# Edge rows stored apart, value products for two query blocks at once, and K and V projected earlier

## The chip, the cores and the metric

One core of one Trainium2 chip runs the whole program. Its engines work side by side, each through its own queue in order: TensorE (PE) multiplies matrices, VectorE (DVE) and ScalarE (ACT) work on elements, GpSimd (POOL) and SyncE (SP) here mainly issue DMA transfers. The metric is device time in microseconds from launch to end, lower is better; it is the median of several executions.

## The reference

Two requests (512 and 256 tokens, 768 in all) pass through two encoder layers with shared weights. All is float32. Cut to what matters:

```
h = rms_norm(x, norm_g);  u = h @ w_in            # 2048 -> 46 column blocks of 128 (and dt)
z, xbc, dt_raw, q, k, v, g_att, hy_proj, g_hy = split(u)
y_ssd = ssd_branch(...)      # conv, two chunked scans (forward, backward), gate z, norm
y_att = attention_branch(...)  # 8 heads, 2 key/value heads, blocks of 128, window 128, bias, sink
y_hy  = hyena_branch(...)    # conv, long filters by Fourier transforms, gate, norm
x = x + concat(y_ssd, y_att, y_hy) @ w_out        # 16 column blocks of 128

# one scan, per chunk of 128 tokens and head
a_cs   = cumsum(dt * a)
y_diag = (C B^T * exp(a_cs_l - a_cs_s) masked) (x dt)
y_off  = (C . state before the chunk) * exp(a_cs)
# attention, per block of 128 queries against up to 3 blocks of keys
p = exp(s - max);  o = (p / (sum p + exp(sink - max))) @ v
```

## The kernel before

**Projections.** A column block is `gemm_col(W(i), f)`: 96 matmuls of 128x384 into two PSUM tiles (`gs`, `gq`), after which `f` takes the result. Each float32 operand is split into a high and a low part and three products are added. The activations' parts (`OPH`, `OPL`) stay in SBUF; the weights arrive on SP's queue (`raw`) and are split chunk by chunk, `hi` on ACT (recorded as L138) and `lo` on DVE (L128), with three buffers each. A chunk feeds 12 matmuls, so PE needs a new `hi` about every 2 us of its wide matmuls, and a late `hi` stops it.

**Background work.** Scan, Fourier filters, hyena and attention are Python generators that the class of `half`, `step`, `later` and `flush` advances between chunks of a column: a `half` step in the middle of a quarter runs due timers (`later`) and the functions that were put in the list `mid`, a whole `step` also advances the generators. `flush(gen)` runs a generator to its end at once. What is written down in this way is then put in an order per engine by the scheduler of the build, which sets the weight splits ahead.

**Scan.** The sixteen heads are handled as eight pairs a layer, beside the xs and hyena columns (W4 to W19). `a_cs` rows are written to `rows_d` in DRAM (six stores a layer, L638) and read back spread over the partitions: `rows` (L684, 256 KB each, six a pair) and, for the four chunks that have a neighbour before or after, `E2` (L726, per direction one load of three chunks, 192 KB, and one of one chunk, 64 KB). Then `xs_d` (L746, 385 KB) follows on the same GpSimd queue. ACT takes the exponent of each `E2`, DVE multiplies it with `Y`; the pair's last stage adds up on DVE `D x + y` and the `E2` terms into `XS`. The shared PSUM tiles `m` have four buffers, so a late `E2` holds `Y`, and with it the next pair's `Y`.

**Later columns.** After the scan come z (W20 to W27), whose squares end in `rms`, and `scale_ssd`, which scales the eight `XS` and stores them to `ys_d` (L1037, 384 KB each). Then the hyena's xa columns (W28 to W31), each behind `bg.flush(hy[j // 2])`; then K (W32), V (W33) and the four Q columns (W34 to W37), beside which attention runs. K's consumer writes `KH` by four ACT copies into the space of `XS` 6 and 7, so those wait for the `ys_d` stores to have read it.

**Attention.** A unit is one block of 128 queries of two heads; there are 24 a layer. They pass a pipeline: `score`, `turn` (transposes on PE), `pv`, which multiplies with the values (four or six instructions in the code, each two records in the trace, of the form 128*64 128x128), with one DVE copy behind it.

Of the kernel before, what the change touches and what calls it, by code (L numbers as in the profile page):

```python
# [11 lines left out]
F32 = mybir.dt.float32  # L12
# [7 lines left out]
DEPTH = 2  # L20
# [77 lines left out]
def trunk(ctx: ExitStack, tc: tile.TileContext, xT, w_in, w_dt, w_out, prm, brow, w1, mlpv, w2, w3, w4,  # L98
# [28 lines left out]
    def TT(o, a, b, op, eng=None):  # L127
        (eng or nc.vector).tensor_tensor(out=o, in0=a, in1=b, op=op)  # L128
# [5 lines left out]
    def STT(o, a, s, b, op0, op1, eng=None):  # L134
        (eng or nc.vector).scalar_tensor_tensor(out=o, in0=a, scalar=s, in1=b, op0=op0, op1=op1)  # L135
# [44 lines left out]
    fb_d = drp.tile([8, 128, 512], F32, name="fb_d")  # L180
    f0_d = drp.tile([8, 512], F32, name="f0_d")
    rows_d = drp.tile([DEPTH, 2, 16, NCH, 128], F32, name="rows_d")
    ys_d = drp.tile([DEPTH, 8, 128, T], F32, name="ys_d")
    xs_d = drp.tile([DEPTH, 8, 128, T + GAP], F32, name="xs_d")

# [2 lines left out]
    def P(l, base, i):  # L188
        c = l * NPRM + base + i
        return prm_t[:, c:c + 1]  # L190
# [413 lines left out]
    def ssd_gen(l, dtT, BT, CT, ready):  # L604
# [22 lines left out]
        TT(adt, dt, bc(na, (128, 2, NCH, 16)), MUL)  # L627
        yield
        yield
        for b in range(3):  # L630
            p = mp((16, 4, 128))
            for i in range(4):
                c, d = divmod(4 * b + i, 2)
                MM(p[:, i, :], adt[:, d, c, :], tri_t[:, d, :])
            r = t2((16, 4, 128))
            nc.scalar.copy(out=r, in_=p)
            for d in range(2):
                load(out=rows_d[l, d, :, 2 * b:2 * b + 2, :],  # L638
                     in_=r.rearrange("h (c d) t -> h d c t", d=2)[:, d])
        p = mp((128, 2, 2, NCH, 16))  # L640
        for d in range(2):
            MM(p[:, 0, d], tri_t[:, d, :], adt[:, d])
# [10 lines left out]
        TS(acs[:, 1], acs[:, 1], -1.0, MUL)  # L653
        yield
        yield

        FW, BW = (0, 1, 2, 4), (1, 2, 3, 5)

        def group(g):
            bt, cbF, cbB = s3((128, NCH, 128)), s3((128, NCH, 128)), s3((128, NCH, 128))  # L660
# [13 lines left out]
        def pair(j, bt, cbF, cbB):  # L674
            g, h0 = j // 4, 2 * j
            Xf = XS(j)
            X = Xf.rearrange("p (c h q) -> p c h q", c=NCH, h=2)
            Ms = []

            def rows(u):  # L680
                R = []
                for d in range(2):
                    t = t2((128, 2, 2, 128))
                    load(out=t, in_=rows_d[l, d, h0:h0 + 2, 2 * u:2 * u + 2, :].partition_broadcast(128))  # L684
                    R.append(t)
                return R

            def prep(u, R):
                Rf, Rb = R
                a1 = t2((128, 2, 2, 128))  # L690
                hc = [(hh, cc, h0 + hh, 2 * u + cc) for hh in range(2) for cc in range(2)]
                for hh, cc, h, c in hc:
                    STT(Rf[:, hh, cc, :], Rf[:, hh, cc, :], acs[:, 0, c, h:h + 1], Rb[:, hh, cc, :], SUB, ALU.min)
                for hh, cc, h, c in hc:
                    ACT(a1[:, hh, cc, :], cbF[:, c, :], AF.Copy, scale=dt[:, 0, c, h:h + 1])
                    ACT(Rb[:, hh, cc, :], cbB[:, c, :], AF.Copy, scale=dt[:, 1, c, h:h + 1])
                    ACT(Rf[:, hh, cc, :], Rf[:, hh, cc, :], AF.Exp, bias=acs[:, 1, c, h:h + 1])
                TT(Rb, Rb, a1, ADD)
                TT(Rf, Rf, Rb, MUL)
                Ms.append(Rf)  # L700

            R0 = rows(0)
            yield
            XW = []
            for d, cs in ((0, FW), (1, BW)):
                o = t2((128, 4, 2, 64))
                for i, n in ((0, 3), (3, 1)):
                    c = cs[i]
                    TT(o[:, i:i + n], X[:, c:c + n], bc(w[:, d, c:c + n, h0:h0 + 2][:, :, :, None], (128, n, 2, 64)), MUL)
                XW.append(o)  # L710
            R1 = rows(1)
            yield
            St = []
            for d, cs in ((0, FW), (1, BW)):
                p = mp((128, 4, 2, 64))
                for i, c in enumerate(cs):
                    MM(p[:, i], bt[:, c, :], XW[d][:, i])
                St.append(p)
            prep(0, R0)
            R2 = rows(2)  # L720
            E2 = []
            for d, cs in ((0, BW), (1, FW)):
                t = t2((128, 4, 128))
                for i, n in ((0, 3), (3, 1)):
                    src = rows_d[l, d, h0:h0 + 2, cs[i]:cs[i] + n, :]
                    load(out=t[:, i:i + n, :], in_=bass.AP(src.tensor, src.offset,  # L726
                         [[NCH * 128, 2], [0, 64], [128, n], [1, 128]]))
                E2.append(t)
            yield
            H = [t2((128, 4, 2, 64)), t2((128, 4, 2, 64))]  # L730
            nc.scalar.copy(out=H[0][:, 0:4:3], in_=St[0][:, 0:4:3])
            nc.scalar.copy(out=H[1][:, 2:4], in_=St[1][:, 2:4])
            for d, seq in ((0, ((1, 0, 1), (2, 1, 2))), (1, ((1, 2, 2), (0, 1, 1)))):
                for o, i, c in seq:
                    for hh in range(2):
                        STT(H[d][:, o, hh, :], H[d][:, i, hh, :], cdec[:, d, c, h0 + hh:h0 + hh + 1], St[d][:, o, hh, :], MUL, ADD)
            prep(1, R1)
            yield
            Y = []
            for d, cs in ((0, BW), (1, FW)):  # L740
                p = mp((128, 4, 128))
                for i, c in enumerate(cs):
                    MM(p[:, i, :], H[d][:, i], CT[g][:, tok(c)])
                Y.append(p)
            t = s3((128, T + GAP))
            load(out=t, in_=xs_d[l, j])  # L746
            prep(2, R2)
            yield
            for d in range(2):
                ACT(E2[d], E2[d], AF.Exp)  # L750
                TT(E2[d], E2[d], Y[d], MUL)
            yield
            yS, yP = mp((128, 4, 128)), mp((128, 2, 128))
            for c in range(NCH):
                for hh in range(2):
                    hs = slice(64 * hh, 64 * hh + 64)
                    o = yS[hs, c, :] if c < 4 else yP[hs, c - 4, :]
                    MM(o, X[:, c, hh, :], Ms[c // 2][:, hh, c % 2, :])
            yield
            dsk = P(l, PDS, j)  # L760
            yT = Xf.rearrange("p (c t) -> p c t", c=NCH)
            STT(yT[:, 0:4], t[:, 0:SL].rearrange("p (c t) -> p c t", c=4), dsk, yS, MUL, ADD)
            STT(yT[:, 4:6], t[:, SL + GAP:T + GAP].rearrange("p (c t) -> p c t", c=2), dsk, yP, MUL, ADD)
            for d, cs in ((0, BW), (1, FW)):
                for i, n in ((0, 3), (3, 1)):
                    c = cs[i]
                    TT(yT[:, c:c + n], yT[:, c:c + n], E2[d][:, i:i + n], ADD)
            yield

        act, nxt, gt = [], 0, None  # L770
# [23 lines left out]
    def att_gen(l, qs, QA, KH, KL, vt):  # L794
# [54 lines left out]
            for (w, _), (p, _) in zip(whole, pw):  # L849
                nc.scalar.copy(out=w, in_=p)  # L850

        def pv(i, tk, kb0, nk, whole, s):
            po = mp((128, 128))
            n = nk // 128
            for kb in range(n):
                for g in range(2):
                    hs = slice(64 * g, 64 * g + 64)
                    MM(po[hs, :], vt[:, kb0 + kb, hs], s[g][:, 128 * kb:128 * kb + 128], kb == 0, kb == n - 1)
            nc.vector.tensor_copy(out=qs[i][:, tk], in_=po)

        pipe = [None] * 4
        for u in units + [None] * 4:
            while u is not None and len(qs) <= u[0]:
                yield
            if pipe[3] is not None:
                pv(*pipe[3])
            if pipe[1] is not None:
                bg.mid.append(lambda p=pipe[1]: turn(*p))
            pipe = [score(*u) if u is not None else None] + pipe[:3]
            yield  # L870
# [96 lines left out]
    for l in range(DEPTH):  # L967
# [68 lines left out]
                TT(y, y, r, MUL)  # L1036
                load(out=ys_d[l, j], in_=y)  # L1037
        rms(acc, 1024, eps4, 2, scale_ssd)
        for j in range(4):
            def f(ps, pq):  # L1040
                bg.flush(hy[j // 2])
                a = hconv(j, ps, pq)
                TT(yh[j][:, 0:SL], yh[j][:, 0:SL], a[:, 0:SL], MUL)
                TT(yh[j][:, SL:T], yh[j][:, SL:T], a[:, SL + GAP:T + GAP], MUL)
            gemm_col(W(28 + j), f)

        new_xs(F32R)
        KH = [XS(6), XS(7)]
        kL = s3p.tile([128, T], F32R, tag="s3", name="kL")
        KL = [(kL[:, 0:SL], kL[:, SL:T]), (t2((128, SL), F32R), t2((128, PL), F32R))]  # L1050

        def f(ps, pq):
            k = s3()
            evac(lambda a, b: k[:, a:b], ps, pq, rstd)
            for g in range(2):
# [10 lines left out]
        def f(ps, pq):  # L1066
# [8 lines left out]
                    nc.scalar.copy(out=vt[:, 3 * b:3 * b + 3, :], in_=p)  # L1075
            bg.later(4, turn)
        gemm_col(W(33), f)
        qs, QA = [], [[XS(2 * i % 6), XS(2 * i % 6 + 1)] for i in range(4)]
        bg.add(att_gen(l, qs, QA, KH, KL, vt))
        for i in range(4):  # L1080
# [193 lines left out]
```

## Time and profile before

| | |
|---|---|
| time, median of 3 runs | 2487.45 us (2485.87 to 2487.83) |
| the profiled execution | 2489.0 us, span 2487.2 us |
| mean granted TensorE clock | 0.993 |
| PE busy | 2441.4 us (98%), 15066 matmul records |
| DVE, ACT, POOL busy | 1580.5, 1087.5, 341.4 us (64%, 44%, 14%) |
| DMA | 266.22 MB, mean 107 GB/s |

The trace is one execution. Its views are: the page; the waits (what ended an engine's idle time); the chain of waits (the work that ended last, followed back); the timeline of one engine, where a row with a count joins equal instructions, and the text in brackets is the idle time just before and what ended it; the DMA issues with the median time from issue to landing; and stretches (windows) with the busy time of each engine and the granted clock of PE (1.00 is 2.4 GHz, 0.50 is 1.2 GHz). The starts on PE are measured, the ends are modelled, so lengths of stretches on PE are taken from start to start.

### The profile page before, as it was taken

How to read it: one execution, taken by the hardware profiler on the slowest of the kernel's cores; microseconds unless marked ns; L12 is line 12 of the kernel's file. 1: busy time of each engine (PE TensorE's matmuls, PEld its weight loads, DVE VectorE, ACT ScalarE, POOL GpSimd, SP SyncE). 2: the span in 40 equal slices, each digit the busy share in tenths (PEclk: the TensorE clock that was granted, in tenths of full speed). 3: DMA queues.
4: the chain of work that ended last, by engine and by line, in shares of the span. 5: the costliest groups of instructions: out<-in, count | busy, mean ns of one | idle time of the engine just before them, and what ended most of it. 6: DMA issues, size and time to landing. Idle time of an engine off the chain costs nothing.

```text
span 2487.2 us, 40924 instructions
## 1 busy us (share of the span) xinstructions
PE 2441.4 (98%) x15066; PEld 2393.2 (96%) x15066; DVE 1580.5 (64%) x3410; ACT 1087.5 (44%) x2560; POOL 341.4 (14%) x683
## 2 busy tenths in 40 slices
PE   8999999999999999999999999999999999999998
PEld 7999999999999999999999999999999999999997
DVE  6888775558856766544476787766746477573333
ACT  6467653334334444333353575633332355352332
POOL 2033221221100010121200332201001000000001
PEclk9999999999999999999999999999999999999999
DMA  4266542443421132344421555423213111332223
GB/s 169 63 153 146 142 129 86 129 133 124 140 78 60 51 100 80 112 149 132 146 96 55 141 149 149 135 85 106 94 60 128 63 54 47 106 109 89 77 82 132
DMA packets 126921, 266.22 MB, mean 107 GB/s; under 512 B 30175, under 2 KB 36666, under 8 KB 126720
## 3 DMA queue, kind: packets, MB, share of 16 engines
q1 hardware_dynamic: 78048, 136.35, 17.7%
q0 software_dynamic: 48672, 127.26, 17.2%
q8 instruction: 118, 1.93, 0.3%
q14 instruction: 83, 0.68, 0.1%
HBM read 231.23 MB, written 34.18 MB: 107 GB/s over the span
## 4 chain that ended last, share of the span: by engine, by line
PE 90%; DMA 4%; issue 2%; DVE 1%; ACT 1%; POOL 1%; DVEq 0%; ACTq 0%; POOLq 0%
PE gs L141 38%; PE gq L141 38%; PE m L141 12%; DMA t<-rows_d 3%; PE m L848 1%; PE gl L141 1%; POOL t L726 0%; ACT t L138 0%; DMA XS<-in_xT 0%; DMA s<-in_xT 0%; ACT hi L138 0%; DVE lo L128 0%; DVE t L135 0%; PE m L1000 0%; DVE t L128 0%
## 5 line engine op out<-in xcount | busy, mean ns | idle before, releaser
L138 ACT ACTIVATE hi<-raw 128x256 fp32r<-128x256 f32 x984 | 405.6, 414 | 1040.1 <-PE gq L141 920.5
L128 DVE TENSOR_TENSOR lo<-raw,hi 128x256 fp32r<-128x256 f32 x984 | 412.5, 421 | 597.9 <-ACT hi L138 587.0
L141 PE MATMUL gs<-OPH,hi 128*128 128x384 f32 x1920 | 657.4, 342 | 18.1 <-ACT OPH L138 11.0
L141 PE MATMUL gs<-OPH,lo 128*128 128x384 f32 x1920 | 645.0, 336 | 0.6 <-DVE lo L128 0.5
L141 PE MATMUL gq<-OPH,lo 128*128 128x384 f32 x1920 | 644.4, 336 | 0.0
L141 PE MATMUL gs<-OPL,hi 128*128 128x384 f32 x1920 | 644.0, 336 | 0.1
L141 PE MATMUL gq<-OPH,hi 128*128 128x384 f32 x1920 | 644.1, 335 | 0.0
L141 PE MATMUL gq<-OPL,hi 128*128 128x384 f32 x1920 | 643.3, 335 | 0.0
L141 PEld LDWEIGHTS gs<-OPH,hi 128*128 128x128 f32 x1920 | 362.4, 189 | 25.2 <-ACT OPH L138 11.3
L141 PEld LDWEIGHTS gs<-OPH,lo 128*128 128x128 f32 x1920 | 361.6, 188 | 2.7 <-DVE lo L128 2.7
L141 PEld LDWEIGHTS gs<-OPL,hi 128*128 128x128 f32 x1920 | 362.3, 189 | 0.8 <-DVE OPL L135 0.6
L141 PEld LDWEIGHTS gq<-OPH,hi 128*128 128x128 f32 x1920 | 361.8, 188 | 0.0
L141 PEld LDWEIGHTS gq<-OPL,hi 128*128 128x128 f32 x1920 | 361.6, 188 | 0.0
L141 PEld LDWEIGHTS gq<-OPH,lo 128*128 128x128 f32 x1920 | 361.5, 188 | 0.0
L128 DVE TENSOR_TENSOR t<-t,t 128x512 f32<-128x512 f32 (+3 forms) x260 | 169.1, 668 | 26.5 <-ACT t L138 23.6
L135 DVE SCALAR_TENSOR_TENSOR s<-cv,prm_t,s 128x770 f32<-128x770 f32 x144 | 145.9, 1015 | 22.6 <-ACT s L138 21.9
L138 ACT ACTIVATE t<-s,dt 128x128 f32<-128x128 f32 x384 | 133.6, 391 | 18.9 <-DVE t L135 18.5
L128 DVE TENSOR_TENSOR s<-s,s 128x768 f32<-128x768 f32 (+2 forms) x126 | 112.8, 904 | 27.3 <-ACT s L138 26.7
L138 ACT ACTIVATE t<-t 128x512 fp32r<-128x512 f32 (+3 forms) x132 | 77.3, 587 | 92.4 <-DMA t<-rows_d 48.6
L128 DVE TENSOR_TENSOR t<-m,t 128x256 f32<-128x256 f32 (+3 forms) x157 | 72.3, 485 | 18.3 <-PE m L141 5.8
L684 POOL DMA_DIRECT2D t<-rows_d x96 | 68.8, 719 | 103.9 <-DVE XS L128 38.0
L138 ACT ACTIVATE t<-t,acs 128x128 f32<-128x128 f32 x192 | 73.6, 389 | 13.6 <-DVE t L135 13.6
(225 smaller groups left out, 2572.6 us busy)
## 6 DMA issues: line engine op xcount, KB each, us to landing
raw<-in_w_in SPq DMA_DIRECT2D x368, 256.0 KB, 3.0
raw<-in_w_out SPq DMA_DIRECT2D x128, 256.0 KB, 3.0
t<-rows_d POOLq DMA_DIRECT2D x96, 256.0 KB, 6.4
s<-in_xT POOLq DMA_DIRECT2D x24, 384.0 KB, 4.4
xs_d<-s POOLq DMA_DIRECT2D x16, 385.0 KB, 4.2
s<-xs_d POOLq DMA_DIRECT2D x16, 385.0 KB, 9.3
t<-rows_d POOLq DMA_DIRECT2D x32, 192.0 KB, 10.5
t<-in_decay POOLq DMA_DIRECT2D x24, 256.0 KB, 4.9
```

The costliest lines, as they stand in the source:

```text
L128: (eng or nc.vector).tensor_tensor(out=o, in0=a, in1=b, op=op)
L135: (eng or nc.vector).scalar_tensor_tensor(out=o, in0=a, scalar=s, in1=b, op0=op0, op1=op1)
L138: nc.scalar.activation(o, i, f, **kw)
L141: nc.tensor.matmul(o, lhsT=l, rhs=r, start=start, stop=stop)
L684: load(out=t, in_=rows_d[l, d, h0:h0 + 2, 2 * u:2 * u + 2, :].partition_broadcast(128))
L848: nc.tensor.transpose(pt[g][:, 128 * kb:128 * kb + 128], s[g][:, 128 * kb:128 * kb + 128], ident)
```

## The change

Five edits in one diff:

- a second DRAM array `ed_d` holds the four edge chunks of each direction; each of the six stores of a layer to `rows_d` gets a second store of one or two chunks beside it;
- an `E2` tile is loaded by two loads of 64 partitions x 2 KB from `ed_d`, one per head, instead of one of three chunks and one of one chunk over 128 partitions;
- the pair's last stage becomes a function in `bg.mid`;
- `pv2` gathers two units, multiplies both into one PSUM tile and copies each out;
- K and V are projected ahead of the xa columns, and `KH` and `KL` are allocated in K's consumer.

```diff
+    ed_d = drp.tile([DEPTH, 2, 16, 4, 128], F32, name="ed_d")
...
+        FW, BW = (0, 1, 2, 4), (1, 2, 3, 5)
         for b in range(3):
...
             for d in range(2):
-                load(out=rows_d[l, d, :, 2 * b:2 * b + 2, :],
-                     in_=r.rearrange("h (c d) t -> h d c t", d=2)[:, d])
+                v = r.rearrange("h (c d) t -> h d c t", d=2)[:, d]
+                load(out=rows_d[l, d, :, 2 * b:2 * b + 2, :], in_=v)
+                cs = [(i, c - 2 * b) for i, c in enumerate((BW, FW)[d]) if c // 2 == b]
+                i, c = cs[0]
+                load(out=ed_d[l, d, :, i:i + len(cs), :], in_=v[:, c:c + len(cs)])
...
-            for d, cs in ((0, BW), (1, FW)):
+            for d in range(2):
                 t = t2((128, 4, 128))
-                for i, n in ((0, 3), (3, 1)):
-                    src = rows_d[l, d, h0:h0 + 2, cs[i]:cs[i] + n, :]
-                    load(out=t[:, i:i + n, :], in_=bass.AP(src.tensor, src.offset,
-                         [[NCH * 128, 2], [0, 64], [128, n], [1, 128]]))
+                for hh in range(2):
+                    load(out=t[64 * hh:64 * hh + 64], in_=ed_d[l, d, h0 + hh].partition_broadcast(64))
...
-            yield
-            dsk = P(l, PDS, j)
...
+            def final():
+                dsk = P(l, PDS, j)
...
+            bg.mid.append(final)
             yield
...
-        def pv(i, tk, kb0, nk, whole, s):
-            po = mp((128, 128))
+        def pv2(us):
+            po = mp((128, len(us), 128))
+            for k, u in enumerate(us):
+                pv(po[:, k], *u)
+            for k, u in enumerate(us):
+                nc.vector.tensor_copy(out=qs[u[0]][:, u[1]], in_=po[:, k])
+
+        def pv(po, i, tk, kb0, nk, whole, s):
...
             if pipe[3] is not None:
-                pv(*pipe[3])
+                done.append(pipe[3])
+                if len(done) == 2:
+                    pv2(done)
+                    done = []
...
-        for j in range(4):
-            def f(ps, pq):
-                bg.flush(hy[j // 2])
...
-            gemm_col(W(28 + j), f)
-
-        new_xs(F32R)
-        KH = [XS(6), XS(7)]
...
+        KH, KL = [], []
 
         def f(ps, pq):
+            new_xs(F32R)
+            KH.extend((XS(6), XS(7)))
...
         gemm_col(W(33), f)
+        for j in range(4):
+            def f(ps, pq):
+                bg.flush(hy[j // 2])
...
+            gemm_col(W(28 + j), f)
+
```

The edits move instructions in three places. The first is attention on PE in layer 0, beside the Q columns; `gs` and `gq` are the wide projection matmuls, `64x128` the value products, `m<-XS`, `m<-kL` and the `128x256` row between or behind them the next unit's scores. Before, every gap between wide matmuls holds one unit's value products and a unit's scores:

```order
L141 MATMUL gq<-OPL,hi 128x384
L141 MATMUL gq<-OPH,lo 128x384
L141 MATMUL m<-t_8202,s_7829 64x128 x4
L141 MATMUL m<-XS 128x256
L141 MATMUL m<-kL,XS 128x256
L141 MATMUL m<-XS 128x256
L141 MATMUL m<-t_7675,XS 128x256
L141 MATMUL gs<-OPH,hi 128x384
```

Now one gap holds scores alone, and the next, one unit later, the value products of two units (four and six instructions) ahead of the scores:

```order
L141 MATMUL gq<-OPH,lo 128x384
L141 MATMUL m<-t_8209,s_6960 64x128 x4
L141 MATMUL m<-t_8263,s_6960 64x128
L141 MATMUL m<-t_8264,s_6960 64x128
L141 MATMUL m<-t_8263,s_6960 64x128
L141 MATMUL m<-t_8264,s_6960 64x128
L141 MATMUL m<-t_8263,s_6960 64x128
L141 MATMUL m<-t_8264,s_6960 64x128
L141 MATMUL m<-XS 128x256
L141 MATMUL m<-kL,XS 128x256
L141 MATMUL m<-XS 128x256
L141 MATMUL m<-t_6944,XS 128x256
```

The first unit's four products have moved to where the second's six stand; 22 gaps of the two layers lose their value products in this way.

The second place is the end of the hyena in layer 0 on PE; `m<-r,t` are the products that transform back into time. Before, the last 48 of them stand in one block behind the last matmul of column W31, ahead of column W32:

```order
L141 MATMUL gq<-OPL,hi 128x384
L141 MATMUL gq<-OPH,lo 128x384
L141 MATMUL m<-r_7436,t_7285 128x256 x2
L141 MATMUL m<-r_7437,t_7285 128x256
L141 MATMUL m<-r_7436,t_7286 128x256
L141 MATMUL m<-r_7436,t_7289 128x256
L141 MATMUL m<-r_7437,t_7289 128x256
```

Now they stand inside the column of W30, with two wide matmuls of it between them:

```order
L141 MATMUL gs<-OPH,hi 128x384
L141 MATMUL m<-r_7499,t_7255 128x256 x2
L141 MATMUL gs<-OPL,hi 128x384
L141 MATMUL gs<-OPH,lo 128x384
L141 MATMUL m<-r_7500,t_7255 128x256
L141 MATMUL m<-r_7499,t_7256 128x256
L141 MATMUL m<-r_7499,t_7259 128x256
L141 MATMUL m<-r_7500,t_7259 128x256
L141 MATMUL m<-r_7499,t_7260 128x256
L141 MATMUL m<-r_7505,t_7487 128x256
L141 MATMUL m<-r_7500,t_7255 128x256
L141 MATMUL m<-r_7506,t_7487 128x256
```

Column W30 is now the fifth behind the z columns where it was the third, so the hyena's generator has come to this stage before its flush.

The third place is the four `KH` copies on ACT in layer 0 (`XS<-s 64x768`) among the weight splits. Before, they stand about three columns behind the `ys_d` stores and wait for what was left of them:

```order
L138 ACTIVATE hi<-raw 128x256 [waits DVE_49,PE_49]
L138 ACTIVATE hi<-raw 128x256 [waits DMAHW5_49,DVE_49,PE_49]
L138 ACTIVATE XS<-s_7814 64x768 [waits DMASW7_49,DMASW0_49,DVE_49]
L138 ACTIVATE XS<-s_7814 64x768
L138 ACTIVATE hi<-raw 128x256 [waits PE_49,Activation_49]
L138 ACTIVATE XS<-s_7814 64x768 x2
L138 ACTIVATE hi<-raw 128x256 [waits DMAHW6_49,PE_49,Activation_49]
```

Now the first of them stands about one column behind the stores and waits for all eight (the eight DMASW semaphores), with the following splits queued behind it:

```order
L138 ACTIVATE hi<-raw 128x256 [waits DMAHW0_49,DVE_49,PE_49]
L138 ACTIVATE hi<-raw 128x256 [waits DVE_49,PE_49]
L138 ACTIVATE XS<-s_6945 64x768 [waits DMASW4_49,DMASW3_49,DMASW5_49,DMASW2_49,DMASW6_49,DMASW1_49,DMASW7_49,DMASW0_49,DVE_49]
L138 ACTIVATE XS<-s_6945 64x768 x2
L138 ACTIVATE hi<-raw 128x256 [waits DMAHW1_49,PE_49,Activation_49]
L138 ACTIVATE XS<-s_6945 64x768
L138 ACTIVATE hi<-raw 128x256 [waits PE_49,Activation_49]
```

What moved is the four copies, two columns ahead, so that the splits of the column behind V now stand behind the wait.

## Rows read from the trace of the kernel before

**Rows 1.** The page, the chain that ended last, by line.

```profile
PE gs L141 38%; PE gq L141 38%; PE m L141 12%; DMA t<-rows_d 3%; PE m L848 1%; PE gl L141 1%; POOL t L726 0%; ACT t L138 0%; DMA XS<-in_xT 0%; DMA s<-in_xT 0%; ACT hi L138 0%; DVE lo L128 0%; DVE t L135 0%; PE m L1000 0%; DVE t L128 0%
```

**Rows 2.** Waits of PE: waiter, releaser, us in total, times, longest.

```profile
PE m L141 <- DVE XS L135: 7.9, 2, 4.0
PE gs L141 <- ACT hi L138: 6.5, 5, 2.1
```

**Rows 3.** Chain of waits, 262 to 280 us: start, us, what.

```profile
264.84 9.33 DMA t<-rows_d
...
275.56 0.75 DVE XS L135
```

**Rows 4.** The E2 loads, line L726: who waited for them, and their landing.

```profile
ACT t L138: 48.6, 24
...
DMA to landing us min/median/max: 5.9/10.3/13.7
```

**Rows 5.** Timeline of PE around column W31's end: start, us, instruction, idle before.

```profile
690.70 0.34 PE L141 MATMUL gq<-OPH,lo 128*128 128x384 f32 x1
695.61 8.94 PE L141 MATMUL m<-r,t 128*128 128x256 f32 x48 [4.58 <-ACT r L138]
704.38 0.34 PE L141 MATMUL gs<-OPH,hi 128*128 128x384 f32 x1
```

**Rows 6.** Windows behind stalls: stretch, length, busy of five engines, PEclk, DMA, GB/s.

```profile
189.90:193.40 3.50, 3.47 (x11) 3.21 (x12) 3.47 (x9) 3.50 (x11) 0.00 (x0) 0.52 0.22 75
276.00:282.00 6.00, 5.64 (x23) 5.64 (x24) 4.84 (x14) 2.75 (x8) 0.72 (x1) 0.50 0.31 84
1528.00:1532.00 4.00, 4.00 (x17) 4.00 (x17) 2.84 (x8) 1.95 (x5) 0.64 (x1) 0.59 0.44 129
```

**Rows 7.** DMA issues of the page: queue, count, KB each, median us to landing.

```profile
t<-rows_d POOLq DMA_DIRECT2D x96, 256.0 KB, 6.4
...
s<-xs_d POOLq DMA_DIRECT2D x16, 385.0 KB, 9.3
...
t<-in_fwS POOLq DMA_DIRECT2D x32, 128.0 KB, 4.2
```

**Rows 8.** DMA issues, 1603 to 1605 us: the last xs_d load.

```profile
s<-xs_d POOLq DMA_DIRECT2D x1, 385.0 KB, 3.6
```

**Rows 9.** Timeline of POOL: the last five rows_d stores of layer 1.

```profile
1370.73 2.51 POOL L638 DMA_DIRECT2D rows_d<-t  x5 [0.92 <-issue]
```

**Rows 10.** Timeline of PE at one unit's and at two units' value products.

```profile
910.97 0.33 PE L141 MATMUL gq<-OPL,hi 128*128 128x384 f32 x1
911.14 0.34 PE L141 MATMUL gq<-OPH,lo 128*128 128x384 f32 x1
911.41 0.66 PE L141 MATMUL m<-t,s 128*64 128x128 f32 x8
...
912.28 0.34 PE L141 MATMUL gs<-OPL,hi 128*128 128x384 f32 x1
...
916.55 0.34 PE L141 MATMUL gq<-OPH,lo 128*128 128x384 f32 x1
916.82 1.13 PE L141 MATMUL m<-t,s 128*64 128x128 f32 x16
...
918.15 0.34 PE L141 MATMUL gs<-OPL,hi 128*128 128x384 f32 x1
```

**Rows 11.** Timeline of PE in column W28: the same products inside a column.

```profile
619.57 5.59 PE L141 MATMUL m<-r,t 128*128 128x256 f32 x46
```

**Rows 12.** Timeline of POOL: the last ys_d store of layer 0.

```profile
646.05 0.54 POOL L1037 DMA_DIRECT2D ys_d<-XS  x1 [0.67 <-PE gq L141]
```

**Rows 13.** The ys_d stores, line L1037: their landing.

```profile
DMA to landing us min/median/max: 3.3/4.8/7.1
```

**Rows 14.** The page: the weight splits on ACT, count, busy, mean ns, idle before.

```profile
L138 ACT ACTIVATE hi<-raw 128x256 fp32r<-128x256 f32 x984 | 405.6, 414 | 1040.1 <-PE gq L141 920.5
```

**Rows 15.** Timeline of PE: the first wide matmul of column W30.

```profile
648.54 0.33 PE L141 MATMUL gs<-OPH,hi 128*128 128x384 f32 x1
```

More of the change, by code (lines that the diff above doesn't have):

```diff
@@ L655, in ssd_gen @@
         yield
-        FW, BW = (0, 1, 2, 4), (1, 2, 3, 5)
         def group(g):
@@ L758, in pair @@
                     MM(o, X[:, c, hh, :], Ms[c // 2][:, hh, c % 2, :])
-            yield
-            dsk = P(l, PDS, j)
[L761 to L767, printed above, removed]
+            def final():
+                dsk = P(l, PDS, j)
+                yT = Xf.rearrange("p (c t) -> p c t", c=NCH)
+                STT(yT[:, 0:4], t[:, 0:SL].rearrange("p (c t) -> p c t", c=4), dsk, yS, MUL, ADD)
+                STT(yT[:, 4:6], t[:, SL + GAP:T + GAP].rearrange("p (c t) -> p c t", c=2), dsk, yP, MUL, ADD)
+                for d, cs in ((0, BW), (1, FW)):
+                    for i, n in ((0, 3), (3, 1)):
+                        c = cs[i]
+                        TT(yT[:, c:c + n], yT[:, c:c + n], E2[d][:, i:i + n], ADD)
+            bg.mid.append(final)
             yield
@@ L858, in pv @@
                     MM(po[hs, :], vt[:, kb0 + kb, hs], s[g][:, 128 * kb:128 * kb + 128], kb == 0, kb == n - 1)
-            nc.vector.tensor_copy(out=qs[i][:, tk], in_=po)
-        pipe = [None] * 4
+        pipe, done = [None] * 4, []
         for u in units + [None] * 4:
@@ L1038, in trunk @@
         rms(acc, 1024, eps4, 2, scale_ssd)
-        for j in range(4):
-            def f(ps, pq):
-                bg.flush(hy[j // 2])
-                a = hconv(j, ps, pq)
-                TT(yh[j][:, 0:SL], yh[j][:, 0:SL], a[:, 0:SL], MUL)
-                TT(yh[j][:, SL:T], yh[j][:, SL:T], a[:, SL + GAP:T + GAP], MUL)
-            gemm_col(W(28 + j), f)
-        new_xs(F32R)
-        KH = [XS(6), XS(7)]
-        kL = s3p.tile([128, T], F32R, tag="s3", name="kL")
-        KL = [(kL[:, 0:SL], kL[:, SL:T]), (t2((128, SL), F32R), t2((128, PL), F32R))]
+        KH, KL = [], []
         def f(ps, pq):
+            new_xs(F32R)
+            KH.extend((XS(6), XS(7)))
+            kL = s3p.tile([128, T], F32R, tag="s3", name="kL")
+            KL.extend(((kL[:, 0:SL], kL[:, SL:T]), (t2((128, SL), F32R), t2((128, PL), F32R))))
             k = s3()
@@ L1077, in trunk @@
         gemm_col(W(33), f)
+        for j in range(4):
+            def f(ps, pq):
+                bg.flush(hy[j // 2])
+                a = hconv(j, ps, pq)
+                TT(yh[j][:, 0:SL], yh[j][:, 0:SL], a[:, 0:SL], MUL)
+                TT(yh[j][:, SL:T], yh[j][:, SL:T], a[:, SL + GAP:T + GAP], MUL)
+            gemm_col(W(28 + j), f)
         qs, QA = [], [[XS(2 * i % 6), XS(2 * i % 6 + 1)] for i in range(4)]
```

## The prediction

> **What bounds the kernel now.** I read the page first, then the waits of PE, then the chain of waits around the longest ones, then the timeline at each place that the diff touches. PE is busy for 98% of the span, and the chain runs through its wide matmuls, with the E2 and row loads as the only other piece above 2% [rows 1]. So an edit pays only if it takes away PE's idle time, the low clock that follows it, or time inside PE's own sequence. The waits name two idle sums to look for [rows 2]: 7.9 us in two waits of the `m` matmuls for DVE's `XS` and 6.5 us in five waits for a weight split. Both lie in the scan: the chain around the longest shows an E2 load issued at 264.84 and landed 9.33 us later, and only behind it, at 275.56, the DVE step that gives back the PSUM tile for which PE waits [rows 3]. The five late splits stand on ACT behind exponents of such tiles: ACT waited 48.6 us for E2 loads, 24 times, for each one the queue behind it [rows 4]. A third place is the end of the hyena in layer 0, where PE waits 4.58 us for ACT's `r` [rows 5].
>
> **E2 from its own array (1).** What the stalls cost: idle 7.9 + 6.5 = 14.4 us [rows 2], and the low clock after them. In three stretches behind stalls PE was busy 3.47, 5.64 and 4.00 us at 0.52, 0.50 and 0.59 of the clock [rows 6], so 3.47 x 0.48 + 5.64 x 0.50 + 4.00 x 0.41 = 6.1 us of work were lost. Together 20.5 us. What the change does to them hangs on the landing of the new loads, which no row shows. The bytes stay 512 KB a pair and the loads four. The nearest row is the load of the same size, 128 KB into SBUF on the same queue, with 4.2 us; the `rows` loads, 256 KB that are spread over partitions, take 6.4 us; today's E2 takes 10.3 us [rows 4, 7]. At 4.2 the E2 of [rows 3] is there 9.33 - 4.2 = 5.1 us earlier, more than the longest wait of 4.0, so all 20.5 us go. At 6.4 it is there 2.9 us earlier, and the two long waits keep about 1.1 us each; the five short ones, at most 2.1 us, go. The `xs_d` load stands behind the E2 loads on the queue and lands 9.3 us after its issue, while the one that was issued with none in flight landed after 3.6 [rows 7, 8], so it comes earlier with them. I take 18 us, near the row of equal size; the ends are 0 (the landing stays) and 20.5, and a loss is a rival below.
>
> The E2 loads of [rows 4] are slow for their size: a transfer twice as large as their 192 KB lands in a third of the time [rows 8]. The Trainium skill (DMA: Bandwidth & Descriptors, "Why a DMA increments its semaphore by 16 and not by 1") gives a reason: the number of DMA engines is the largest count up to 16 that divides the slowest dimension of both sides, and in today's source that dimension is the 2 heads, in the new one the 64 partitions. By that rule today's loads use 2 engines and the new ones 16, the whole 20.5 us would go, and the sum below would end 2.5 us lower.
>
> **Twelve more stores and `final` (2).** A store of `rows_d` holds POOL for 2.51 / 5 = 0.50 us [rows 9], so six more a layer delay the first pair's `rows` loads by 3.0 us. Two layers bound this at 0 and 6 us, and I take 1, since before the first pair PE has had no wait that the rows name. `final` keeps its place on DVE to within two rows of the order; it frees nothing sooner that PE waits for: 0, bounds -1 and 1.
>
> **Two units at once (3).** A run of 8 narrow records costs 912.28 - 911.14 = 1.14 us from one wide start to the second one behind it, a run of 16 costs 918.15 - 916.55 = 1.60 [rows 10]. Two single runs are 2.28, one double run and the two wide pitches of 0.17 that stand apart from it are 1.60 + 0.34 = 1.94: each merge gives 0.34 us. Where scores follow, the way into the narrow form and out of it is paid once less too. 22 merges give 7.5; I take 7.0, since most gaps hold scores whose own first matmul is longer. These are PE's own microseconds, nothing hides them. The copies stay 48, but come in pairs; PE waits for none of them with four `m` buffers, or else the gain shrinks to 0 (the other bound).
>
> **K and V first (4).** The block of 48 `m<-r,t` stands alone between two columns: from 690.70 to 704.38 are 13.68 us [rows 5]. 46 of the same products inside a column take 5.59 us [rows 11], so 48 take 5.83, and with one pitch of 0.17 the place costs 13.68 - 5.83 - 0.17 = 7.7 us too much, of which 4.58 are the named wait and the rest splits that come one behind another and a low clock. In the new order these products stand inside column W30 as those of [rows 11] do, two columns of work later than their data. I take 7.5; bounds 4.6 (the rest stays) and 7.7.
>
> The move also adds a wait. In layer 0 the four `KH` copies on ACT now need all eight `ys_d` stores, and the splits for the second column behind V queue behind them. The last store is issued at 646.05 [rows 12] and lands after 4.8, at most 7.1 us [rows 13]: at 650.9 or 653.2. Two of the copies and a split come next; that they take together about 2 us is an estimate from the 0.41 us that ACT takes for a split of 256 columns [rows 14] and the threefold width of the copies. That puts the split at 653 to 655. The column that starts at 648.54 [rows 15] needs this one two chunks later, and a chunk is 12 x 0.17 = 2.0 us: 652.6. PE would wait 0 to 2.5 us, and a low clock could add as much again. I take 1, bounds 0 and 5. In layer 1 the same copies stand further behind the stores: 0.
>
> **The sum.** -18 + 1 - 7.0 - 7.5 + 1 = -30.5 us. The profiled execution took 2489.0 us, 1.8 more than its span; 2489.0 - 30.5 = 2458.5. The median of the runs is 1.5 below the profiled one, so I forecast **2457 us**.
>
> **Rivals.** (a) *The landing stays.* The loads move the same bytes over the same queue at the same moment, when `rows`, weights and the `xs_d` store are in flight; if that crowd sets the 10.3 us, the stalls of the scan stay. The crowd is real, since `rows` loads too take 6.4 us where 128 KB alone takes 4.2; but 3.6 us for 385 KB speaks against it [rows 7, 8]. Term (1) falls to 0: 2489.0 + 1 - 7.0 - 7.5 + 1 - 1.5 = 2475 us. The Trainium skill (DMA: Bandwidth & Descriptors, "Specifications") has transfers at line rate from pieces of 512 B up; E2's pieces are three rows of 512 B already, so that by this rule longer ones gain nothing, which is this rival.
> (b) *`KH` holds ACT longer.* All eight stores and the weights cross at once, and K's column lies closer to them in both layers. At 5 us in each, 9 more than taken, it gives 2466 us. Against it, the longest landing of a store is 7.1 us [rows 13].
> (c) *Slower.* The new loads let 64 partitions read one 2 KB row at the same time. If they land as late as today's latest, 13.7 us instead of 10.3 [rows 4], each of the seven scan waits grows by 3.4 us, 24 us in all, in place of the 18 gained: 2457 + 18 + 24 = 2499 us. It is slower than before once the other gains of 12.5 us are used up, from a landing of 10.3 + 12.5 / 7 = 12.1 us. Against it, the `rows` loads let 128 partitions read one row and land in 6.4 us.
> (d) *The merge gives nothing.* If the first unit's later product holds its PSUM tile or its exponents too long, term (3) is 0: 2464 us. The order shows the merged runs, so that it does not happen at all is excluded.
>
> **How the numbers follow.** The forecast with its own range (2452 with all bounds at their best, 2463 with the E2 landing nearer 6.4 us and 3 us of new waits) has 0.66; (b) 0.12; (d) 0.05; (a) 0.13; (c) 0.04. The range must reach (b) and (d) and, to leave out no more than 2 in 10, most of (a): 2448 (a further 4 us, if waits that the rows do not name go too) to 2475. A measurement of this kernel tells about 0.2% from no change, 5 us: the same is 2482.5 to 2492.4. No case centres there; between (a) and (c) lies 0.03. Slower is (c), 0.04; faster 0.93.
>
> **What would show it.** Right: the E2 loads land in 4 to 6 us; the 7.9 us wait for `XS` is gone or under 2 us and the waits for `hi` shrink to 1 or 2; no block of `m<-r,t` stands between two columns; two units' records stand in one run with 1.4 to 1.6 us around it. Wrong: the `t<-ed_d` landing at 8 us or more (a, c); ACT idle at K's copies while PE waits for `hi` (b); new waits of PE for `t` or `s` in the Q columns (d).

## The result and the profile after

The changed kernel takes **2450.56 us** (median, 2449.24 to 2452.37) beside 2487.34 for the kernel before: a ratio of 0.9854, with a 95% interval of 0.9837 to 0.9871, or 36.8 us less. The forecast was 2457 us, 2448 to 2475. The profiled execution of after spans 2447.9 us, 39.3 less than that of before; some 2.5 us of this, 1.2 of them ahead of the first scan column, are spread between executions, so stages are compared by trace and totals by medians.

The page of the kernel after, its parts on engines, on the chain by line and on DMA:

```profile
PE 2421.7 (99%) x15066; PEld 2385.4 (97%) x15066; DVE 1581.0 (65%) x3410; ACT 1090.0 (45%) x2560; POOL 327.9 (13%) x695
...
DMA packets 113993, 266.12 MB, mean 109 GB/s; under 512 B 16927, under 2 KB 23546, under 8 KB 113792
...
PE gs L141 39%; PE gq L141 39%; PE m L141 12%; PE m L850 1%; PE gl L141 1%; DMA t<-rows_d 1%; DMA t<-in_fwS 0%; DMA t<-in_w 0%; PE m L1010 0%; DMA prm_t<-in_prm 0%; ACT t L138 0%; DVE dt L135 0%; PE m L502 0%; DVE s L135 0%; POOL XS L1128 0%
```

The matmul records are the same 15066, PE's busy time is 19.7 us shorter (2441.4 before): time at the low clock and time in the narrow runs counted as busy. On the chain the loads have fallen from 3% to 1% [rows 1]. The waits of PE (waiter, releaser, us in total, times, longest):

```profile
PE gs L141 <- ACT OPH L138: 10.8, 2, 9.7
PE m L141 <- DVE t L128: 1.9, 1, 1.9
PE m L141 <- DVE s L128: 1.1, 1, 1.1
PE m L141 <- ACT t L852: 0.9, 1, 0.9
PE m L141 <- ACT t L138: 0.7, 1, 0.7
...
```

Both sums of [rows 2] are gone, and so is the wait for `r` of [rows 5]. The first row is the start of the program, as before. New is the wait for DVE's `t`, 1.9 us; it is taken up below. E2's own rows, who waited for line L728 and its landing:

```profile
ACT t L138: 2.3, 4
...
DMA to landing us min/median/max: 2.7/6.6/9.6
```

Against [rows 4], ACT waits 2.3 us in place of 48.6. The issues on the page (KB each, median us to landing):

```profile
t<-rows_d POOLq DMA_DIRECT2D x96, 256.0 KB, 6.1
...
t<-ed_d POOLq DMA_DIRECT2D x64, 128.0 KB, 6.6
...
s<-xs_d POOLq DMA_DIRECT2D x16, 385.0 KB, 6.4
```

By the medians E2 lands as `rows` does, and `xs_d` behind it comes 2.9 us sooner [rows 7]. But the median of 6.6 us stands between two groups. In eight of the sixteen pairs at least four `rows` loads are issued in the 8 us ahead of E2, and E2 lands after 7.6 to 9.6 us; in the other eight it lands after 2.7 to 5.6. The issues of one pair of either group, the third (191.5 to 193.6 us) and the fifth (255.9 to 258) of layer 0:

```profile
t<-ed_d POOLq DMA_DIRECT2D x4, 128.0 KB, 9.6
...
t<-ed_d POOLq DMA_DIRECT2D x4, 128.0 KB, 4.1
```

In the kernel before, the five waits of 1.4 us or more that PE had in the scans came right after the late landing of E2 of the second, fifth and eighth pair of layer 0 and of the fifth and eighth of layer 1. All five pairs are now in the fast group. The place of [rows 3], on PE's timeline of after, now without a wait between the column's last wide matmul (265.26) and the next column's first (267.79), 2.53 us where 8.43 stood before (271.36 to 279.79):

```profile
265.26 0.34 PE L141 MATMUL gq<-OPH,lo 128*128 128x384 f32 x1
265.43 0.82 PE L1010 MATMUL m<-ident,s 128*128 128x128 f32 x6
266.08 1.95 PE L141 MATMUL m<-t,s 128*128 128x128 f32 x16
267.79 0.42 PE L141 MATMUL gs<-OPH,hi 128*128 128x384 f32 x1
```

**Where the time went, by stage.** The stages run from the first wide matmul of one column to that of another, read from PE's timeline of each trace; columns of layer 0 in the first four rows, of layer 1 in the others (its attention from the third Q column, W36, on); differences to before in us. The stages that are not listed differ by 0.3 at most, but for the time ahead of W4 of layer 0 (the changed kernel -1.2; the other kernels -1.4 to +0.2). The single edits are the first four experiments below.

| stage | before | changed | E2 only | final only | pv2 only | K, V only |
|---|---|---|---|---|---|---|
| W4 to W16, scan | 270.7 | -13.8 | -14.2 | -2.9 | -1.6 | -1.4 |
| W16 to W28, end of hyena | 240.3 | -2.6 | +2.2 | -1.8 | -0.1 | +0.1 |
| W28 to Q, xa, K, V | 131.5 | -3.1 | +0.1 | -1.9 | -0.9 | -3.2 |
| Q to the last gate, attention | 214.9 | -3.4 | +0.9 | +0.9 | -3.4 | -0.4 |
| layer 1, scan | 264.1 | -10.9 | -10.9 | +1.1 | +0.3 | -1.6 |
| layer 1, W16 to W28 | 235.7 | -0.5 | 0.0 | -0.4 | 0.0 | 0.0 |
| layer 1, attention | 179.2 | -4.1 | 0.0 | -0.1 | -4.0 | -0.2 |

In the last three columns E2 is still late, and the scan differs by 0.3 to 3 us from trace to trace; where it is not late, the scan of layer 1 repeats to a tenth.

### The profile page after: what moved, and what is told of

Read it like the earlier page. It is cut to its first block, busy times and chain, and to the rows that moved or that the text cites. A ratio compares the mean times of both kernels' runs of the same rounds, so it can differ in the third digit from the quotient of the medians.

```text
span 2447.9 us, 40978 instructions
## 1 busy us (share of the span) xinstructions
PE 2421.7 (99%) x15066; PEld 2385.4 (97%) x15066; DVE 1581.0 (65%) x3410; ACT 1090.0 (45%) x2560; POOL 327.9 (13%) x695
## 2 busy tenths in 40 slices
DMA packets 113993, 266.12 MB, mean 109 GB/s; under 512 B 16927, under 2 KB 23546, under 8 KB 113792
## 4 chain that ended last, share of the span: by engine, by line
PE 92%; issue 3%; DMA 2%; DVE 1%; POOL 1%; ACT 1%; DVEq 0%; POOLq 0%; ACTq 0%
PE gs L141 39%; PE gq L141 39%; PE m L141 12%; PE m L850 1%; PE gl L141 1%; DMA t<-rows_d 1%; DMA t<-in_fwS 0%; DMA t<-in_w 0%; PE m L1010 0%; DMA prm_t<-in_prm 0%; ACT t L138 0%; DVE dt L135 0%; PE m L502 0%; DVE s L135 0%; POOL XS L1128 0%
## 5 line engine op out<-in xcount | busy, mean ns | idle before, releaser
L141 PE MATMUL gs<-OPH,hi 128*128 128x384 f32 x1920 | 655.3, 341 | 10.8 <-ACT OPH L138 10.8
```

The costliest lines, as they stand in the source:

```text
L141: nc.tensor.matmul(o, lhsT=l, rhs=r, start=start, stop=stop)
```

## Experiments

Each kernel was timed beside the kernel before on one chip; medians are given with the ratio to before and its 95% interval.

### One edit at a time

**e2_only.** The kernel before with the hunks of `ed_d`, its stores and its loads:

```diff
+                load(out=ed_d[l, d, :, i:i + len(cs), :], in_=v[:, c:c + len(cs)])
...
+                    load(out=t[64 * hh:64 * hh + 64], in_=ed_d[l, d, h0 + hh].partition_broadcast(64))
```

> The kernel before with the E2 edit alone (ed_d stores and loads; the pair's last stage and everything else as before). Theory A, the landing of E2 is what stalled the scan: t<-ed_d lands in about 6.6 us, the time from the first matmul of W4 to that of W16 falls from 270.7 to about 257 us and in layer 1 (W4 to W16) from 264.2 to about 253, in all 2487.3 - 24 = 2463 us. Rival B, the function in bg.mid (one stage less per pair) does a good part of it: the scan gains less than 12 us, over 2475.

Measured: 2465.19 us beside 2486.84, ratio 0.9911 (0.9894 to 0.9927), -21.7 us. Both scans gain what they gain in the changed kernel. Theory A. The 2.2 us that W16 to W28 lose here come with a stretch in which PE's granted clock falls (0.69 from 489.0 to 494.5 us); neither before nor the changed kernel has one there.

**final_only.** The kernel before with the last stage deferred:

```diff
-            yield
-            dsk = P(l, PDS, j)
+            def final():
+                dsk = P(l, PDS, j)
...
+            bg.mid.append(final)
             yield
```

> The kernel before with the pair's last stage in bg.mid alone. Theory A: the order moves by a few rows only and E2 lands as late as before, so within 3 us of 2487. Rival B: each pair's loads start a step earlier and the scan gains 5 us or more, 2482 or less.

Measured: 2482.06 us beside 2486.84, ratio 0.9980 (0.9971 to 0.9990), -4.8 us. More than A allowed, and not where B has it: 3.7 us lie behind the scan (W16 to Q), and the two scans together give 1.8 with E2 as late as ever.

**pv2_only.** The kernel before with `pv2`:

```diff
+                done.append(pipe[3])
+                if len(done) == 2:
+                    pv2(done)
+                    done = []
```

> The kernel before with pv2 alone. Theory A, a fixed price of 0.34 us for each run of value products: 22 runs fewer give 7.5 us, 2480, all of it between the first Q column and the end of the attention gates of each layer. Rival B: part of the 7.5 us that these stages gained in the changed kernel came with the other edits, so less than 4 us here.

Measured: 2479.01 us beside 2486.84, ratio 0.9970 (0.9956 to 0.9984), -7.8 us; the attention stages give 3.4 + 4.0 = 7.4. Theory A.

**kv_only.** The kernel before with K and V ahead of the xa columns, `KH` allocated in K's consumer:

```diff
         gemm_col(W(33), f)
+        for j in range(4):
+            def f(ps, pq):
+                bg.flush(hy[j // 2])
```

> The kernel before with K and V ahead of the xa columns alone. Theory A: the block of 48 transform products between two columns is gone (-7.7 us) and the KH copies on ACT hold splits that the hyena's products need (+4): -3 to -4 us, 2484. Rival B: KH comes late only because the other edits put the hyena earlier; then here the whole 7 us show, 2480.

Measured: 2483.32 us beside 2486.84, ratio 0.9988 (0.9978 to 0.9997), -3.5 us, 3.2 of them between W28 and Q. Theory A: the move costs its own wait, with or without the other edits.

The four add up to 21.7 + 4.8 + 7.8 + 3.5 = 37.8 us; the whole gives 36.8. In the sum the edits hardly touch each other; by stage they do: from W28 to Q the deferral alone gives 1.9 and K and V alone 3.2, all edits together 3.1.

**final_undone.** The changed kernel with the last stage as a stage of its own again:

```diff
-            def final():
-                dsk = P(l, PDS, j)
+            yield
+            dsk = P(l, PDS, j)
...
-            bg.mid.append(final)
             yield
```

> The changed kernel with the pair's last stage as before (a stage of its own, not in bg.mid). Theory A: the deferral lets everything behind the scan run a step earlier, which gave 3.7 us in the filter and xa columns of final_only; these come back, 2454. Rival B: what it gave in final_only (4.8 us) was cover for late E2 loads, which the changed kernel no longer has; 2450.6 within 1.5.

Measured: 2453.47 us beside 2486.95, ratio 0.9870 (0.9856 to 0.9883); 2.9 us over the changed kernel. By stages, W16 to W28 takes 3.3 us longer than in the changed kernel (+0.7 to before, against -2.6), the scans the same. So the deferral's gain is not cover for E2: it lies in the hyena and filter work behind the scan. The waits of PE from W16 to W28 in layer 0, first of final_undone, then of the changed kernel:

```profile
PE m L141 <- ACT t L138: 2.3, 2, 1.6
PE gs L141 <- DVE s L128: 0.6, 1, 0.6
PE m L502 <- DVE r L128: 0.6, 1, 0.6
...
```

```profile
PE m L141 <- ACT t L138: 0.7, 1, 0.7
```

With a fourth row of 0.4 us, the first kernel waits 3.9 us there and the changed one 0.7: that is the difference between the stages. The stage is one `yield` shorter for each pair, so the generators behind the scan can run a step earlier; that it is this step and not the place of `final` itself was not tried apart.

### What made E2 late

The forecast took a landing of 4.2 to 6.4 us from other loads and left open what sets it. The edit changed two things, the length of the runs and the shape of the source.

**e2_split_src.** The kernel before, loaded from `rows_d` in the old runs, but one head at a time:

```diff
-                    src = rows_d[l, d, h0:h0 + 2, cs[i]:cs[i] + n, :]
-                    load(out=t[:, i:i + n, :], in_=bass.AP(src.tensor, src.offset,
-                         [[NCH * 128, 2], [0, 64], [128, n], [1, 128]]))
+                        load(out=t[64 * hh:64 * hh + 64, i:i + n, :],
+                             in_=rows_d[l, d, h0 + hh, cs[i]:cs[i] + n, :].partition_broadcast(64))
```

> The kernel before, whose E2 tiles are loaded from rows_d as before (runs of 1.5 KB and 0.5 KB) but one head at a time: eight loads a pair of 64 partitions each, so that the slowest dimension of the source is 64 and no longer 2. No ed_d, nothing else changed. Theory A, the two-head source made the loads slow: E2 lands in about 7 us and most of the scan's gain is here, 2463 to 2470 us, the rest lost to four more issues a pair on GpSimd. Rival B, the runs of the source must be long and contiguous: landing stays near 10 us, 2487 or more.

Measured: 2467.16 us beside 2487.15, ratio 0.9920 (0.9906 to 0.9935), -20.0 us. Theory A in the time, though the loads land sooner than it said. The scan of layer 1 gains its 10.9 us, that of layer 0 10.8 of 14.2. Its DMA issues:

```profile
s<-xs_d POOLq DMA_DIRECT2D x16, 385.0 KB, 4.1
t<-rows_d POOLq DMA_DIRECT2D x64, 96.0 KB, 3.9
t<-rows_d POOLq DMA_DIRECT2D x64, 32.0 KB, 3.9
```

**e2_pair_ap.** The changed kernel, loaded from `ed_d` in runs of 2 KB, but both heads in one load:

```diff
-                for hh in range(2):
-                    load(out=t[64 * hh:64 * hh + 64], in_=ed_d[l, d, h0 + hh].partition_broadcast(64))
+                src = ed_d[l, d, h0:h0 + 2]
+                load(out=t, in_=bass.AP(src.tensor, src.offset, [[4 * 128, 2], [0, 64], [128, 4], [1, 128]]))
```

> The changed kernel, whose E2 tiles are loaded from ed_d in runs of 2 KB as there, but both heads in one load of 128 partitions (source: 2 heads, 64 times each, 2 KB): two loads a pair of 256 KB. Theory A, the two-head source made the loads slow: landing about 10 us again, the scan's stalls come back, 2465 to 2475 us. Rival B, contiguity was it: landing 6.6 us or less with half the issues, 2450 or less.

Measured: 2482.70 us beside 2487.15, ratio 0.9976 (0.9966 to 0.9986). It loses 32 us against the changed kernel, more than A said: the scans take 9.6 us longer than even before. The bytes and the 2 KB runs are those of the changed kernel; what differs is that one load of 128 partitions takes two rows where two loads of 64 take one each. Its issues and the waits of PE:

```profile
t<-ed_d POOLq DMA_DIRECT2D x32, 256.0 KB, 10.7
...
s<-xs_d POOLq DMA_DIRECT2D x16, 385.0 KB, 10.6
```

```profile
PE gs L141 <- ACT hi L138: 12.7, 7, 4.9
...
PE m L141 <- DVE XS L135: 7.8, 2, 4.0
```

The landing of before, the waits of [rows 2] (with 12.7 us instead of 6.5) and a late `xs_d` are back. In the five pairs behind PE's longer waits E2 took 6.0 to 13.7 us before; it takes 7.5 to 11.6 here, 2.3 to 7.1 in e2_split_src and 2.8 to 5.3 in the changed kernel. The size of a load is not what makes it late, since the `rows` loads, 256 KB over 128 partitions too, land after 6.1 us in this kernel. So the two heads in one source made the load slow; contiguous runs and the second array did not make it fast. The page's count of packets shows the same split: under 512 B there are 30175 in the kernel before and 30751 here, 16927 in the changed kernel and 17759 in e2_split_src, whose page says:

```profile
DMA packets 115658, 266.00 MB, mean 108 GB/s; under 512 B 17759, under 2 KB 25210, under 8 KB 115456
```

With the two-head source some 13 thousand more packets of under 512 B go with these loads (8 to 32 B each in the traces), whatever the length of the runs. Whether these packets or a small number of DMA engines make the load late, no run separates. Which engines carried the packets the trace does not record. The Trainium skill (DMA: Bandwidth & Descriptors, "Why a DMA increments its semaphore by 16 and not by 1") says that as a rule the slowest dimension of both sides sets how many DMA engines a transfer uses; the four landings (10.5 and 10.7 us with 2, 3.9 and 6.6 us with 64) agree with it, and no run shows the engines themselves. The same page's 512 B as the least for line rate ("Specifications") is not tested: in e2_split_src the load in runs of 0.5 KB landed as soon as that in runs of 1.5 KB, but it moves a third of the bytes.

### The wait that K and V brought

In the changed kernel the four `KH` copies held ACT. Its timeline there:

```profile
632.09 2.57 ACT L138 ACTIVATE XS<-s 64x768 fp32r<-64x768 f32 x3 [2.90 <-DMA t<-in_fwS]
634.68 0.42 ACT L138 ACTIVATE hi<-raw 128x256 fp32r<-128x256 f32 x1
635.12 0.84 ACT L138 ACTIVATE XS<-s 64x768 fp32r<-64x768 f32 x1
```

DVE's timeline behind it, where K's low parts (`kL`, `t<-s,XS`) wait for these copies, and PE's:

```profile
632.97 2.05 DVE L128 TENSOR_TENSOR kL<-s,XS 64x512 fp32r<-64x512 f32 x4 [2.35 <-ACT XS L138]
...
635.59 1.73 DVE L128 TENSOR_TENSOR t<-s,XS 64x512 fp32r<-64x512 f32 x3
...
639.51 0.69 DVE L128 TENSOR_TENSOR t<-t,t 128x512 fp32r<-128x512 f32 x1
```

```profile
640.25 0.51 PE L141 MATMUL m<-r,t 128*128 128x256 f32 x2 [1.87 <-DVE t L128]
```

The last `ys_d` store was issued at 626.35, and two loads for the hyena (`t<-in_fwS`), which the profile names as the releaser, at 626.88 and 627.42. The DMA issues of 626.2 to 627.95 have the landings:

```profile
t<-in_fwS POOLq DMA_DIRECT2D x2, 256.0 KB, 6.5
ys_d<-XS POOLq DMA_DIRECT2D x1, 384.0 KB, 5.4
```

The store landed at 631.8, just ahead of the copies (632.09), the loads at 633.2 and 634.1, behind their start: it was the store that they waited for. ACT was then late by a little, but DVE, which waited 2.35 us for the copies, had thirteen operations of K, V and the weight splits in line from 632.97 on, ahead of the split of a transform matrix (639.51), for which PE waited 1.87 us in the middle of a column. A window of 640 to 645 us has the granted clock at 0.66 with PE busy for 4.75, another 4.75 x 0.34 = 1.6 us:

```profile
636.00:640.00 4.00, 2.31 (x14) 1.67 (x12) 3.91 (x9) 1.24 (x3) 0.00 (x0) 1.00 0.18 61
640.00:645.00 5.00, 4.75 (x20) 4.75 (x21) 2.64 (x7) 1.47 (x4) 0.00 (x0) 0.66 0.18 60
```

**kv_second.** The changed kernel with one xa column ahead of K and V:

```diff
+        xa(0)
         KH, KL = [], []
...
         gemm_col(W(33), f)
-        for j in range(4):
+        for j in range(1, 4):
+            xa(j)
```

> The changed kernel with K and V one column later (first xa column, K, V, then the other three). Theory A: the KH copies then stand a column behind the ys_d stores and hold up nothing, the 48 transform products still stand inside a column: the 4 us that the changed kernel lost at 632 to 645 us go, 2447. Rival B: what PE lost there belongs to the hyena's own loads and chain (t<-in_fwS landed at 632.1), so no change, 2450 to 2452.

Measured: 2447.08 us beside 2487.15, ratio 0.9839 (0.9823 to 0.9856), 3.5 us under the changed kernel. W28 to Q gains 7.3 us against before instead of 3.1, and PE has no wait there at all. ACT's timeline shows the copies start without one:

```profile
643.77 0.42 ACT L138 ACTIVATE hi<-raw 128x256 fp32r<-128x256 f32 x1 [3.64 <-PE gq L141]
644.22 1.72 ACT L138 ACTIVATE XS<-s 64x768 fp32r<-64x768 f32 x2
645.96 0.42 ACT L138 ACTIVATE hi<-raw 128x256 fp32r<-128x256 f32 x1
```

Theory A in the time. The run alone does not exclude B, since the hyena's loads moved too: they are issued at 643.63 here, 16.8 us behind the last store (626.88) and no longer right behind it. What speaks against them is the trace of the changed kernel, where they landed before ACT had finished with the copies and took up the split of a transform (636.62).

### Further, and together

**pv4.** The changed kernel with four units in one PSUM tile:

```diff
-                if len(done) == 2:
+                if len(done) == 4:
```

> The changed kernel with the value products of four units in one PSUM tile (one bank) instead of two. Theory A, a fixed price per run: 12 runs fewer x 0.34 = 4.1 us, 2446.5. Rival B: three units' exponents and the PSUM tile are held longer and PE waits for tiles in the Q columns, 2450 or more.

Measured: 2445.23 us beside 2487.15, ratio 0.9832 (0.9818 to 0.9847), 5.3 us under the changed kernel; its attention stages give 2.6 + 2.2 = 4.8 us more than the changed kernel's. In layer 0, PE's wait of 0.87 us for ACT's `t` (L852) is gone and one of 0.3 for a `lo` has come; the other 4.2 are 12 runs at 0.35. Between W28 and Q it gains another 1.7 us: its trace has no stretch at the low clock there. On PE's timelines a gap with two units (changed kernel) and one with four (pv4):

```profile
862.28 0.34 PE L141 MATMUL gq<-OPH,lo 128*128 128x384 f32 x1
862.55 1.09 PE L141 MATMUL m<-t,s 128*64 128x128 f32 x16
863.58 0.38 PE L141 MATMUL m<-XS 128*128 128x256 f32 x1
```

```profile
801.28 0.34 PE L141 MATMUL gq<-OPH,lo 128*128 128x384 f32 x1
801.55 2.19 PE L141 MATMUL m<-t,s 128*64 128x128 f32 x36
803.67 0.39 PE L141 MATMUL m<-XS 128*128 128x256 f32 x1
```

From wide start to score start 16 records take 1.30 us and 36 take 2.39: 20 more for 1.09, so 0.054 each, and 1.30 - 16 x 0.054 = 0.43 is what a run costs beside its records, of which 0.17 is the wide matmul's own pitch. Theory A.

**kv_second_pv4.** Both edits.

> The changed kernel with both further edits, K and V one column later and four units in one PSUM tile. Theory A, they act at different places: 2450.6 - 3.5 - 5.3 = 2442. Rival B, pv4 owes part of its 5.3 us to the xa columns, where kv_second acts too (by stages 1.7 us): 2443.5 to 2445.

Measured: 2442.88 us beside 2486.95, ratio 0.9826 (0.9813 to 0.9839). It beats both kernels, 7.7 us under the changed one; the 1 us to the sum is too small to choose between A and B. By stage B's point holds: W28 to Q gains 7.3 us, no more than with kv_second alone, so the 1.7 of pv4 are not added again.

**no_ed.** The same without `ed_d`, with E2 as in e2_split_src:

> kv_second_pv4 without ed_d: E2 from rows_d as in e2_split_src, one head at a time in runs of 1.5 KB and 0.5 KB, eight loads a pair, and six stores a layer instead of twelve. Theory A: with loads of one head the second array is of no use, 2442 within 2 us. Rival B: four more issues a pair on GpSimd push rows and xs_d back and the scan stalls as in e2_split_src (layer 0 gained 10.8 us there against 14.2), 2445 or more.

Measured: 2443.92 us beside 2486.95, ratio 0.9830 (0.9817 to 0.9843), as fast as kv_second_pv4. Theory A: once a load takes one head, neither the second array nor the six more stores a layer are needed. One column of layer 0 (W8) takes 3.4 us longer in its trace (24.11 us start to start against 20.75), and others less. e2_split_src shows the same (24.72); PE waits 2.0 us for DVE's `t` in the scans of both, and at most 0.5 in kv_second_pv4. So it goes with the eight issues a pair; by which way was not followed up.

## Why the prediction was right

**The order of the terms, and the sum.** 36.8 us were measured and 30.4 forecast (2487.45 to 2457). The time lies below the forecast's own range (2452 to 2463), in the 4 us that were added below it for waits that the rows do not name. What took it there were two terms of the sum, with 6.7 and 3.9 us more than taken; a third gave 3.4 less. That these partly cancel is luck. Each term against its stage:

- **E2 (1): 18 taken, 24.7 in the changed kernel's scans, 21.7 by the time of e2_only.** The landing was forecast between 4.2 and 6.4 us and came out at 6.6 in the median, with eight of the pairs at 7.6 to 9.6, about the forecast's own sign of being wrong; the waits went all the same, since the pairs behind them are of the fast group (3.9 to 4.4 us at the place of [rows 3], for which the forecast took 4.2). That the pairs that count would be the fast ones was not foreseen. What was mis-sized was the price of the stalls, 20.5 us, which was also taken as the end of the term's range. PE's idle time in the two scans fell by 14.8 us, as counted (14.4). The windows of the two scans, before and then after (length, PE busy, clock in the third column from the right), give the rest:

```profile
95.16:365.84 270.68, 262.25 (x1695) 254.11 (x1695) 216.04 (x520) 171.97 (x471) 78.35 (x148) 0.98 0.53 135
1352.71:1616.86 264.15, 257.35 (x1688) 251.89 (x1688) 206.31 (x505) 161.47 (x462) 76.06 (x141) 0.99 0.53 139
```

```profile
93.96:350.85 256.89, 256.57 (x1695) 250.37 (x1695) 218.22 (x523) 172.00 (x471) 72.21 (x155) 1.00 0.53 145
1328.62:1581.86 253.24, 253.11 (x1687) 248.92 (x1687) 207.84 (x505) 163.13 (x462) 69.64 (x147) 1.00 0.53 145
```

  The same matmuls took 5.7 and 4.2 us less busy time, 9.9 where three stretches behind stalls [rows 6] had given 6.1. A fourth stretch at the low clock was left out:

```profile
1606.00:1610.00 4.00, 4.00 (x16) 4.00 (x15) 2.02 (x7) 4.00 (x15) 0.00 (x0) 0.57 0.34 117
```

  It adds 4.00 x 0.43 = 1.7 us, 7.8 in all, and the scans of before have no fifth; the other 2.1 us of busy time no row names. Start to start of the columns would have given the sum at once.
- **Stores and `final` (2): -1 taken, 2.9 gained.** This step failed, beyond its bounds. The stores cost nothing that shows (by the median they land after 2.3 and 2.4 us, and the scan of e2_only gains fully). `final` was costed at 0 because its own place on DVE did not move; what it gave are waits of PE behind the scan, 3.9 us that fell to 0.7 (final_undone).
- **Two units at once (3): 7.0 taken, 7.5 measured by stage, 7.8 alone.** Right, with the price per run from [rows 10]. One new wait of 0.87 us stands at the last pair, for ACT's copy of the second unit's exponents, in layer 0.
- **K and V (4): 7.5 gained and 1 lost were taken; 3.1 remain by stage, 3.5 alone.** The 7.5 was right: kv_second shows 7.3 without the new wait. The new wait was mis-sized: about 4 us where 1 was taken, within its bounds of 0 and 5. It was sought in the weight splits, and ACT did queue them; but PE was held by DVE, two engines on, where K's low parts, V's evacuation and a transform's split stood in one line.

**The rivals.** (a) fell: the landing did not stay. Its ground, that the crowd on the queue sets the landing, fell for the pairs behind PE's longer waits, by e2_split_src and e2_pair_ap. It did not fall altogether: behind a row of `rows` loads the new loads too take 7.6 to 9.6 us. (b) was half there, in layer 0 only, by 3 of the 9 us. (c) fell with the landing, and (d) with pv2_only. What the forecast lacked was the cause of the late landing; it would have weighed against (a) and (c) ahead of the run, and shown a smaller edit.

## What to carry to other kernels

When a load lands late, look first at how its source is described: a broadcast over partitions whose outermost dimension is 2 is better issued as two loads, and neither a second copy in DRAM nor longer runs will replace that. Price stalls from start to start of equal pieces of work, in which idle time, the slow clock behind it and what no row names are all contained; and look at the landings of the transfers that were waited for, not at the median of all. And when a step is deferred or a column moved, follow what else the same queue or generator runs behind it: here a "free" deferral gave 2.9 us, and a column that was moved for its neighbour's sake cost 4 through two engines, until it was moved one column less.

## What the runs showed of the hardware

- A load of 128 partitions from two rows (2 heads, 64 times each) landed in 10.5 to 10.7 us, with runs of 1.5 KB as of 2 KB; the same bytes as loads of 64 partitions from one row landed in 3.9 and 6.6 us (3.9 with eight issues a pair, between which GpSimd waited 23.0 us in 27 places; the landing counts from each issue). About 13 thousand more packets of under 512 B a program went with the first form.
- The same load of 128 KB landed after 2.7 to 5.6 us in eight pairs of the changed kernel and after 7.6 to 9.6 in the eight in which at least four `rows` loads of 256 KB had been issued in the 8 us ahead.
- The late form also delays what is queued behind it: the 385 KB `xs_d` load landed after 9.3 and 10.6 us behind it, after 4.1 and 6.4 behind the other form.
- A run of narrow matmuls between wide ones costs 0.26 to 0.34 us beyond its records, by [rows 10] and by the runs of 16 and 36.
